# Hybrid encoder trunk, two layers: weight tiles split once per layer, kept in DRAM and reloaded as two parts

## The chip, the core and the metric

The kernel runs on one core of one Trainium2 chip. The metric is device time in microseconds (us) from the first to the last instruction; the kernel before takes 4894.8 us (median of three runs).

## What is computed

An encoder trunk of two layers runs over two sequences of 1024 tokens and 1024 channels. For each layer and each sequence:

```
h     = rms_norm(x, g_pre) * (1 + scale) + shift
proj  = h @ w_in
o_a   = mla_mixer(...) * silu(z_a)        # attention
o_b   = rwkv7_mixer(...)                  # a scan per direction
o_c   = mamba2_mixer(...)                 # chunked scan per direction
o_d   = gated_deltanet_mixer(...)         # chunked delta rule per direction
mixed = concat(o_a, o_b, o_c, o_d)
x     = x + gate * rms_norm(mixed @ w_out, g_post)
```

`shift`, `scale` and `gate` come from a conditioning vector through `w_ada`. `w_in` is repacked on the host to 32 tiles of 128 columns (1024 x 128 numbers each), `w_out` is 1024 x 1024. All inputs and outputs are float32.

## The kernel before, in words

**Units.** A unit is one sequence in one layer; there are four, in the order (sequence 0, layer 0), (1, 0), (0, 1), (1, 1). Each unit has an input projection (`stage_in`), the four mixers, and an output projection (`stage_out`; `stage_out_last` in the last unit). The projections work on halves of 512 tokens. The input projection of the next unit and the output projection of the one before are laid beside the mixers of a unit, so the projections fill TensorE while the mixers' chains run on all engines. Projections of P go through DRAM: `in_tile` stores each 128 x 512 result to the tensor P, from which the mixers load.

**Products of two halves.** Both projections multiply float32 numbers as sums of two parts. The activations are kept as `hh` (a rounded part, type float32r) and `hl` (the rest), made once for a token half. The weights are made into `wh` and `wl` in the same way by `split_w` (lines 324 to 330): a cast on ScalarE (line 327, `wh`) and a subtraction on VectorE (line 329, `wl`). Three products are summed: wh x hh, wh x hl and wl x hh.

**Weight tiles.** One load brings 128 partitions x 512 numbers (256 KB) into a buffer `w`, of which there are two. For `w_in` (`in_tile`, lines 301 to 322) this is half a tile of 128 columns, so two loads, two splits and 24 products of 512 columns for each result; for `w_out` (`out_tiles`, lines 332 to 349) it is a quarter of the rows for 256 columns, with 24 products of 256 columns. `wh` and `wl` have three buffers each. A load has to wait until the split two before it has read its buffer; a split has to wait until TensorE has used the split three before it.

**How often.** Every unit and both token halves load and split all weights of the layer again: 4 units x 2 halves x 64 parts of `w_in` = 512 and 4 x 2 x 16 of `w_out` = 128, so 640 splits for 160 different parts.

**Order of the work.** The instructions are emitted in program order with priorities, and a planner of the framework orders each engine's queue by a simulated timeline. `urgent()` gives the split instructions and the eviction of a result a priority ahead of everything else; `spread`, `behind` and `ahead` spread the priorities of projection steps over those of the mixers. Each engine then runs its queue strictly in that order, and all loads and stores are issued by SyncE (line 144), which waits for a buffer or for data before it issues and holds all that follows it. `paced` (line 458) lets TensorE begin a group of 5 or 8 projection products only after the group before has begun, by way of a tiny write of GpSimd (line 462).

The mixers' lines that are named later: 522 to 537 invert triangular blocks on VectorE (transposes at 522 and 537, the update steps `iT` at 529 and `SC` or `iR` at 530), 551 and 558 merge them on TensorE, and 629 to 640 are a short convolution.

Of the kernel before, what the change touches and what calls it, by code (L numbers as in the profile page):

```python
# [10 lines left out]
F32 = mybir.dt.float32  # L11
F32R = mybir.dt.float32r
# [9 lines left out]
D = 1024  # L22
MIX = 1800
EA = 60
GK = 4
GB = 3
# [4 lines left out]
GL = 3  # L31
# [77 lines left out]
class Body:  # L109
    def __init__(self, ctx, tc, A, outs, sl=None):  # L110
        self.tc, self.nc, self.A, self.outs = tc, tc.nc, A, outs
        self.n = 0
        self.side = "left"
        self.span = None
        nc = tc.nc
        self.cp = ctx.enter_context(tc.tile_pool(name="cp", bufs=1))
        self.dr = ctx.enter_context(tc.tile_pool(name="dr", bufs=1, space=DRAM))
        self.banks = 3
        self.held = None
        self.token = self.t(self.cp, [1, 1], tag="token")  # L120
        self.gate, self.run = None, 0
        self.ident = self.const(self.cp, "ident")
        self.blk = self.const(self.cp, "blk")
        self.bsel = self.const(self.cp, "bsel")
        self.cc = self.t(self.cp, [128, 4], tag="cc")
        nc.vector.memset(self.cc[:, 0:1], -0.5)
        nc.vector.memset(self.cc[:, 1:2], EPS)
        nc.vector.memset(self.cc[:, 2:3], 0.5)
        nc.vector.memset(self.cc[:, 3:4], 1.0)
        self.mhalf, self.eps, self.phalf, self.one1 = (self.cc[:, i:i + 1] for i in range(4))  # L130

    def open_io(self, ctx):
        """the pools of the projections"""
        self.pj = self.pool(ctx, "pj")
        self.sp = self.pool(ctx, "sp", 2)
        self.pps = self.pool(ctx, "pps", 2, PSUM)
# [20 lines left out]
    def sumsq(self, ps, col, sq, n, rhs, w, start=True, stop=True):  # L157
        """ps[:, col:col+w] = per-token sums over the channels of sq[:, 128 n : 128 n + 128]"""
        for x in range(2):
            self.nc.tensor.matmul(ps[64 * x:64 * x + 64, col:col + w], sq[:, n * 128 + 64 * x:n * 128 + 64 * x + 64], rhs,  # L160
                                  start=start, stop=stop)
# [99 lines left out]
    def stage_in(self, s, L, l, xsrc, Pd, parts=((0, W_ORDER), (1, W_ORDER))):  # L261
        """parts: (token half, tiles); the half of the part before is still there"""
        for hf, names in parts:
            if self.held is None or self.held[0] != (Pd, hf):
                self.spread()
                hh = self.t(self.pj, [128, 8, 512], F32R, tag="hh")
                hl = self.t(self.pj, [128, 8, 512], F32R, tag="hl")
                self.norm_in(s, L, xsrc, hf, hh, hl)
                self.held = (Pd, hf), hh, hl
            for name in names:  # L270
                self.spread()
                self.in_tile(l, name, hf, *self.held[1:], Pd)
# [28 lines left out]
    def in_tile(self, l, name, hf, hh, hl, Pd):  # L301
# [4 lines left out]
        for k in range(8):  # L306
            if k % 4 == 0:
                w = self.t(pj, [128, 4, 128], tag="w", bufs=2)
                self.dma(w, self.A["w_in"][l, ci][:, k * 128:k * 128 + 512].rearrange("p (k c) -> p k c", k=4))
            if k % GK == 0:  # L310
                with self.urgent():
                    wh, wl = self.split_w(w[:, k % 4:k % 4 + GK], [128, GK, 128])
            for i, (a, b) in enumerate(((wh, hh), (wh, hl), (wl, hh))):
                self.paced(TK, ps[0:M], a[:, k % GK, 0:M], b[:, k, :], dict(start=(k == 0 and i == 0), stop=(k == 7 and i == 2)))
# [9 lines left out]
    def split_w(self, w, shape):  # L324
        nc, pj = self.nc, self.pj
        wh = self.t(pj, shape, F32R, tag="wh", bufs=GB)
        nc.scalar.copy(wh, w)  # L327
        wl = self.t(pj, shape, F32R, tag="wl", bufs=GL)
        nc.vector.tensor_tensor(wl, w, wh.bitcast(F32), SUB)  # L329
        return wh, wl  # L330

    def out_tiles(self, l, ch, hh, hl, kqs, at=lambda kq: kq):
        """products of 4 token tiles with a quarter of the columns of w_out, over the quarters kqs of its rows"""
        nc, pj = self.nc, self.pj
        pss = [self.t(self.pps, [128, 2, 256], tag="pj") for _ in range(2)]
        for n, kq in enumerate(kqs):
            w = self.t(pj, [128, 2, 256], tag="w", bufs=2)
            self.dma(w, self.A["w_out"][l, ch, kq // 2][:, (kq % 2) * 512:(kq % 2) * 512 + 512].rearrange("p (k c) -> p k c", k=2))
            with self.urgent():
                wh, wl = self.split_w(w, [128, 2, 256])  # L340
            for i in range(4):
                ps = pss[i // 2][:, i % 2]
                c = slice(i * 128, (i + 1) * 128)
                for k in range(2):
                    a, b = hh[:, at(kq) * 2 + k, c], hl[:, at(kq) * 2 + k, c]
                    first, last = n == 0 and k == 0 and i % 2 == 0, n == len(kqs) - 1 and k == 1
                    for m, (u, w2) in enumerate(((a, wh), (a, wl), (b, wh))):
                        self.paced(TO, ps, u, w2[:, k], dict(start=first and m == 0, stop=last and m == 2, skip_group_check=True))
# [51 lines left out]
    def stage_out_last(self, s, L, l, xsrc, od, dst, parts, ctx=None):  # L400
        """the last output in parts (token half, quarters of the rows of w_out, whether the sums begin or end),
        while the mixers of the later quarters still run"""
# [53 lines left out]
    def paced(self, n, *mm):  # L456
        """a matmul of a bulk stream: groups of n, each issued after the group before has begun"""
# [21 lines left out]
    def behind(self, p0, p1, n, fs):  # L479
        """emit fs with priorities spread over those from p0 to p1"""  # L480
# [34 lines left out]
    def invert(self, pool, r, d, src):  # L515
        """r = inverses of the unit triangular 32 x 32 diagonal blocks of src, transposed"""
# [15 lines left out]
    def merge(self, pool, psp, r, d, src, dst):  # L532
        """dst = inverse of the unit triangular 64 x 64 blocks of src from the inverses r of their diagonal blocks"""
# [33 lines left out]
    def pair_t(self, psp, dst, src, scale=None):  # L567
        """dst[(c parity, t), (c // 2, x, e)] = transposes of 8 chunks of both heads of src, times scale[(c parity, t), c // 2, x]"""
# [9 lines left out]
    def dma_pair(self, dst, src, swap):  # L578
        """dst[(x or 1 - x, t), c, e] (DRAM) = src[(c parity, t), (c // 2, x, e)]"""
# [6 lines left out]
    def head_sum(self, ps, sq, n):  # L586
        """ps[half, i] = sums over the channels of the head of the other half"""
# [4 lines left out]
    def heads_back(self, psp, y):  # L592
        """transposes back to channels: y[(1 - x, t), c, pr, e] -> [(pr, e), x, c, t]"""
# [5 lines left out]
    def rows2(self, t, r0, q):  # L599
        """rows r0 to r0 + 256 and quarter q of the tokens"""  # L600
        return t[r0:r0 + 256, q * 256:q * 256 + 256].rearrange("(r p) t -> p r t", r=2)
# [54 lines left out]
    def rwkv_norm(self, p, psp, L, Pd, q, y, yd, bon, od, free):  # L656
        """normalisation, bonus and gate of a quarter of the tokens"""
# [416 lines left out]
    def gdn_norm(self, p, psp, L, Pd, q, y, yd, fq, od, free):  # L1074
        """normalisation and gate of a quarter of the tokens"""
# [422 lines left out]
    def attend(self, p, psp, qd, kd, krd, VO, ot):  # L1498
        """softmax of every head; the maxima of a head are found during the head before"""
# [74 lines left out]
    def mixers(self, L, Pd, l, od, which="dcab"):  # L1574
        """the streams right (d, a) and left (b, c)"""
# [9 lines left out]
    def last_mixers(self, L, Pd, l, od, io):  # L1585
        """three streams: d, c on the right; b; a in the place of the projections"""
# [16 lines left out]
    def full(self):  # L1603
# [32 lines left out]
        def ahead(w, n, f):  # L1636
            """emit f with priorities spread over the next w, n steps"""
# [87 lines left out]
```

## Time and profile before

| | |
|---|---|
| Runs | 4888.07, 4894.8, 4915.18 us |
| Span of the profiled execution (first to last instruction) | 4894.9 us |
| Instructions | 100724 |
| TensorE products / weight loads | 38644 each |
| Mean granted TensorE clock | 0.878 of full speed |
| DMA traffic | 671.79 MB, mean 137 GB/s |
| HBM read / written | 486.53 / 178.57 MB |

The profile's page comes from one execution, whose own time is its span, 4894.9 us; nothing else around it is shown. PE is TensorE, PEld its weight loads (they overlap the products), DVE VectorE, ACT ScalarE, POOL GpSimd, SP SyncE, and a q behind a name is the engine's sequencer, which waits and issues. In a group of instructions "out<-in" are the program's tile names, and behind the bar stand the busy time in us, the mean of one in ns, and the idle time of the engine just before these instructions with what ended it. The chain that ended last is followed back from the last instruction: at each step to what released it, or to the instruction before it on its engine. A wait "A <- B" means that A stood until B was done. Products are pipelined: two that follow each other start 0.23 us apart though each is shown for 0.39 us.

### The profile page before, as it was taken

How to read it: one execution, taken by the hardware profiler on the slowest of the kernel's cores; microseconds unless marked ns; L12 is line 12 of the kernel's file. 1: busy time of each engine (PE TensorE's matmuls, PEld its weight loads, DVE VectorE, ACT ScalarE, POOL GpSimd, SP SyncE). 2: the span in 40 equal slices, each digit the busy share in tenths (PEclk: the TensorE clock that was granted, in tenths of full speed). 3: DMA queues.
4: the chain of work that ended last, by engine and by line, in shares of the span. 5: the costliest groups of instructions: out<-in, count | busy, mean ns of one | idle time of the engine just before them, and what ended most of it. 6: DMA issues, size and time to landing. Idle time of an engine off the chain costs nothing.

```text
span 4894.9 us, 100724 instructions
## 1 busy us (share of the span) xinstructions
PE 4389.3 (90%) x38644; PEld 3358.2 (69%) x38644; DVE 3343.1 (68%) x6837; ACT 2178.9 (45%) x4734; POOL 397.6 (8%) x2093
## 2 busy tenths in 40 slices
PE   6879798999997988999989898899989989898997
PEld 3667576766776776756767667776767766776686
DVE  2488877566578787566459778657546968856666
ACT  2444363563434534443454453455344354344333
POOL 0101010000101000000011100000011100000001
PEclk8889898998997987989989798798889979878788
DMA  4444264242453546363345353545145535455224
GB/s 144 136 148 138 99 192 132 87 131 99 135 171 126 160 127 192 109 197 110 112 154 162 109 174 117 174 139 147 63 133 165 163 111 158 130 181 156 85 86 137
DMA packets 495063, 671.79 MB, mean 137 GB/s; under 512 B 149752, under 2 KB 265976, under 8 KB 493560
## 3 DMA queue, kind: packets, MB, share of 16 engines
q1 hardware_dynamic: 494584, 665.36, 43.6%
q8 instruction: 306, 5.01, 0.4%
q14 instruction: 173, 1.42, 0.1%
HBM read 486.53 MB, written 178.57 MB: 136 GB/s over the span
## 4 chain that ended last, share of the span: by engine, by line
PE 49%; DVE 13%; DMA 10%; issue 3%; ACT 3%; SPq 1%; POOL 0%; DVEq 0%; POOLq 0%; ACTq 0%
PE pj L458 21%; PE b L824 3%; PE b L1568 2%; PE b L551 2%; DVE iA L522 1%; PE b L558 1%; SPq L144 1%; PE b L1456 1%; PE b L1555 1%; PE pj L243 1%; PE w L863 1%; DVE wl L329 1%; DVE GT L537 1%; PE b L1524 1%; PE y L1220 1%
## 5 line engine op out<-in xcount | busy, mean ns | idle before, releaser
L458 PE MATMUL pj<-hh,wl 128*128 128x512 f32 (+1 forms) x2048 | 848.2, 415 | 32.0 <-DVE wl L329 18.4
L458 PE MATMUL pj<-hh,wh 128*128 128x512 f32 (+1 forms) x2048 | 854.6, 418 | 11.9 <-DVE iT L529 3.2
L458 PE MATMUL pj<-hl,wh 128*128 128x512 f32 (+1 forms) x2048 | 849.7, 415 | 16.9 <-POOL token L462 16.6
L327 ACT CAST wh<-w 128x512 fp32r<-128x512 f32 x640 | 395.1, 618 | 775.4 <-PE pj L458 495.1
L329 DVE TENSOR_TENSOR wl<-w,wh 128x512 fp32r<-128x512 f32 x640 | 446.6, 699 | 245.3 <-ACT wh L327 211.8
L458 PEld LDWEIGHTS pj<-hh,wl 128*128 128x128 f32 (+1 forms) x2048 | 397.5, 194 | 137.5 <-issue 20.7
L458 PEld LDWEIGHTS pj<-hh,wh 128*128 128x128 f32 (+1 forms) x2048 | 397.6, 194 | 115.3 <-issue 19.9
L458 PEld LDWEIGHTS pj<-hl,wh 128*128 128x128 f32 (+1 forms) x2048 | 396.9, 194 | 113.0 <-POOL token L462 22.9
L462 POOL MEMSET token<- 1x1 f32 x1613 | 143.7, 89 | 3317.1 <-PE pj L458 3307.1
L458 PE MATMUL pj<-wh,hl 128*128 128x256 f32 x896 | 266.6, 310 | 0.7 <-DVE hl L363 0.5
L458 PE MATMUL pj<-wh,hh 128*128 128x256 f32 x768 | 238.7, 311 | 6.3 <-ACT hh L362 4.1
L1559 ACT ACTIVATE pT<-b 128x512 f32<-128x512 f32 x256 | 149.8, 596 | 210.6 <-PE b L1557 207.4
L458 PE MATMUL pj<-wl,hh 128*128 128x256 f32 x768 | 234.0, 305 | 0.0
L294 PE MATMUL pj<-c_ident,x 128*128 128x128 f32 x416 | 118.8, 388 | 109.9 <-ACT hh L298 41.0
L1525 DVE TENSOR_REDUCE mx<-b 128x1 f32<-128x512 f32 x256 | 169.7, 686 | 68.5 <-PE b L1524 66.8
L638 DVE SCALAR_TENSOR_TENSOR cva<-cvi,cw,cva 128x1024 f32<-128x1024 f32 x144 | 183.9, 1279 | 47.4 <-ACT cva L634 29.3
L458 PEld LDWEIGHTS pj<-wh,hl 128*128 128x128 f32 x896 | 181.3, 207 | 14.2 <-issue 6.2
L296 ACT ACTIVATE ht<-pj,shc,gsc 128x256 f32<-128x256 f32 x208 | 118.4, 569 | 156.6 <-PE pj L294 84.0
L828 DVE SCALAR_TENSOR_TENSOR G<-b,Dk,mk 128x128 f32<-128x128 f32 x512 | 143.8, 344 | 61.9 <-PE b L824 61.1
L1568 PEld LDWEIGHTS b<-VO,pT 128*64 128x64 f32 x4096 | 150.2, 151 | 42.6 <-issue 29.4
L824 PE MATMUL b<-AR,BK 64*64 64x128 f32 x2048 | 176.7, 299 | 0.0
L1568 PE MATMUL b<-VO,pT 128*64 128x65 f32 x4096 | 168.4, 238 | 4.7 <-ACT pT L1559 4.3
(403 smaller groups left out, 9407.1 us busy)
## 6 DMA issues: line engine op xcount, KB each, us to landing
w<-w_in SPq DMA_DIRECT2D x512, 256.0 KB
P<-st SPq DMA_DIRECT2D x248, 256.0 KB
x<-x SPq DMA_DIRECT2D x76, 512.0 KB
w<-w_out SPq DMA_DIRECT2D x128, 256.0 KB
G<-P SPq DMA_DIRECT2D x112, 256.5 KB
cvi<-P SPq DMA_DIRECT2D x48, 512.0 KB
f<-acr SPq DMA_DIRECT2D x32, 512.0 KB
bkc<-bkd SPq DMA_DIRECT2D x64, 256.0 KB
```

The costliest lines, as they stand in the source:

```text
L294: nc.tensor.transpose(ps[:, i * 128:(i + 1) * 128], xs[i][:, k * 128:(k + 1) * 128], self.ident)
L296: nc.scalar.activation(ht, ps[:, 0:256], AF.Identity, scale=L.gsc[:, k, s:s + 1], bias=L.shc[:, k, s:s + 1])
L327: nc.scalar.copy(wh, w)
L329: nc.vector.tensor_tensor(wl, w, wh.bitcast(F32), SUB)
L458: m = self.nc.tensor.matmul(*mm[:3], **mm[3]).ins
L462: t = self.nc.gpsimd.memset(self.token, 0.0).ins
L638: nc.vector.scalar_tensor_tensor(a, c[:, j:j + 1024], wt(j, i), a, MUL, ADD)
L824: nc.tensor.matmul(ps[self.half(x ^ a), i * 128:i * 128 + 128], BK[self.half(x), pr, c, a], AR[self.half(x), pr, c].rearrange("p a t -> p ...
L828: v.scalar_tensor_tensor(G[:, x, pr, c, :], ps[:, i * 128:i * 128 + 128], Dk[:, c, 2 * x + pr:2 * x + pr + 1], mk, MUL, MUL)
L1525: v.tensor_reduce(mx[:, n, qt:qt + 1], ps, AX.X, ALU.max, negate=True)
L1559: nc.scalar.activation(pT[kt], ps, AF.Exp)
L1568: nc.tensor.matmul(po[64 * x:64 * x + 64, i, :], pT[kt][:, o:o + 64], VO[:, kt, h, :], start=(kt == 0 and i == 0), stop=(kt == 7), skip_gr ...
```

## The change

`split_w` goes. A new function `halves` gives both parts of a weight part in one tile `w2` (128 partitions x 2 x 512, 512 KB; three buffers, the same room as `wh` and `wl` had). The first user in a layer loads `w`, splits it into `w2` as before, and stores `w2` to DRAM. Every other user (the other token half, the other sequence) loads `w2` from there. The products, their order and `paced` stay as they are. Which use is the first follows the order of emission: the units 0 and 2 hold all 160 first uses, spread over both of their token halves, and the units 1 and 3 have none. Other lines of the diff only take out comments.

```diff
-GK = 4
-GB = 3
-GL = 3
...
         self.held = None
+        self.kept = {}
+        self.wd = {(n, l): self.t(self.dr, [m, 128, 2, 512], tag=f"w{n}{l}") for l in range(DEPTH) for n, m in (("in", 2 * NWT), ("out", 16))}
...
         for k in range(8):
             if k % 4 == 0:
-                w = self.t(pj, [128, 4, 128], tag="w", bufs=2)
-                self.dma(w, self.A["w_in"][l, ci][:, k * 128:k * 128 + 512].rearrange("p (k c) -> p k c", k=4))
-            if k % GK == 0:
-                with self.urgent():
-                    wh, wl = self.split_w(w[:, k % 4:k % 4 + GK], [128, GK, 128])
-            for i, (a, b) in enumerate(((wh, hh), (wh, hl), (wl, hh))):
-                self.paced(TK, ps[0:M], a[:, k % GK, 0:M], b[:, k, :], dict(start=(k == 0 and i == 0), stop=(k == 7 and i == 2)))
+                w2 = self.halves(("in", l, ci, k // 4), lambda: self.A["w_in"][l, ci][:, k * 128:k * 128 + 512]).rearrange("p u (k c) -> p u k c", k=4)
+            for i, (a, b) in enumerate(((0, hh), (0, hl), (1, hh))):
+                self.paced(TK, ps[0:M], w2[:, a, k % 4, 0:M], b[:, k, :], dict(start=(k == 0 and i == 0), stop=(k == 7 and i == 2)))
...
-    def split_w(self, w, shape):
+    def halves(self, key, src):
         nc, pj = self.nc, self.pj
-        wh = self.t(pj, shape, F32R, tag="wh", bufs=GB)
-        nc.scalar.copy(wh, w)
-        wl = self.t(pj, shape, F32R, tag="wl", bufs=GL)
-        nc.vector.tensor_tensor(wl, w, wh.bitcast(F32), SUB)
-        return wh, wl
+        w2 = self.t(pj, [128, 2, 512], F32R, tag="w2", bufs=3)
+        wf = w2.bitcast(F32)
+        if key in self.kept:
+            self.dma(wf, self.kept[key])
+            return w2
+        w = self.t(pj, [128, 512], tag="w", bufs=2)
+        self.dma(w, src())
+        with self.urgent():
+            nc.scalar.copy(w2[:, 0], w)
+            nc.vector.tensor_tensor(w2[:, 1], w, wf[:, 0], SUB)
+        kept = self.wd[key[:2]]
+        self.kept[key] = kept[key[2] * 2 + key[3]] if key[0] == "in" else kept[key[2] * 4 + key[3]]
+        self.dma(self.kept[key], wf)
+        return w2
...
         for n, kq in enumerate(kqs):
-            w = self.t(pj, [128, 2, 256], tag="w", bufs=2)
-            self.dma(w, self.A["w_out"][l, ch, kq // 2][:, (kq % 2) * 512:(kq % 2) * 512 + 512].rearrange("p (k c) -> p k c", k=2))
-            with self.urgent():
-                wh, wl = self.split_w(w, [128, 2, 256])
+            w2 = self.halves(("out", l, ch, kq), lambda: self.A["w_out"][l, ch, kq // 2][:, (kq % 2) * 512:(kq % 2) * 512 + 512]).rearrange("p u (k c) -> p u k c", k=2)
...
-                    for m, (u, w2) in enumerate(((a, wh), (a, wl), (b, wh))):
-                        self.paced(TO, ps, u, w2[:, k], dict(start=first and m == 0, stop=last and m == 2, skip_group_check=True))
+                    for m, (u, x) in enumerate(((a, 0), (a, 1), (b, 0))):
+                        self.paced(TO, ps, u, w2[:, x, k], dict(start=first and m == 0, stop=last and m == 2, skip_group_check=True))
```

## Rows read from the trace of the kernel before

**Rows 1.** The page: span; busy time of each engine, share of the span, instructions.
```profile
span 4894.9 us, 100724 instructions
...
PE 4389.3 (90%) x38644; PEld 3358.2 (69%) x38644; DVE 3343.1 (68%) x6837; ACT 2178.9 (45%) x4734; POOL 397.6 (8%) x2093
```

**Rows 2.** The page, the chain that ended last, by engine, then by line.
```profile
...
PE 49%; DVE 13%; DMA 10%; issue 3%; ACT 3%; SPq 1%; POOL 0%; DVEq 0%; POOLq 0%; ACTq 0%
PE pj L458 21%; PE b L824 3%; PE b L1568 2%; PE b L551 2%; DVE iA L522 1%; PE b L558 1%; SPq L144 1%; PE b L1456 1%; PE b L1555 1%; PE pj L243 1%; PE w L863 1%; DVE wl L329 1%; DVE GT L537 1%; PE b L1524 1%; PE y L1220 1%
```

**Rows 3.** Groups by line: shapes and count, busy us and mean ns, idle before.
```profile
...
L329 DVE TENSOR_TENSOR wl<-w,wh 128x512 fp32r<-128x512 f32 x640 | 446.6, 699 | 245.3 <-ACT wh L327 211.8 <-PE pj L458 23.7 <-PE b L571 2.5
...
L327 ACT CAST wh<-w 128x512 fp32r<-128x512 f32 x640 | 395.1, 618 | 775.4 <-PE pj L458 495.1 <-DMA w<-w_in 189.0 <-issue 32.9
```

**Rows 4.** Waits, whole span: engine, line, waited for, us in total, times, longest.
```profile
...
ACT wh L327 <- PE pj L458: 495.1, 273, 9.4
...
DVE wl L329 <- ACT wh L327: 211.8, 151, 7.5
...
ACT wh L327 <- DMA w<-w_in: 189.0, 94, 8.7
```

**Rows 5.** Stretches from 360, 1440, 1680, 2640, 2880, 3840, 4080: all engines; L329 alone.
```profile
...
sum 840.00, PE 740.32 PEld 596.53 DVE 768.81 ACT 330.87 POOL 90.76; mean PE 105.76 PEld 85.22 DVE 109.83 ACT 47.27 POOL 12.97
...
sum 840.00, DVE 111.24; mean DVE 15.89
```

**Rows 6.** The chain from 3850 to 3920: shares by line; pieces (start, us, what).
```profile
...
by line: PE pj L458 35.3%; DVE wl L329 9.9%; DVE iT L529 9.8%; issue 9.3%; DVE SC L530 8.9%; PE yd L1347 5.8%; DMA w<-w_in 4.1%; DVE f L1328 3.6%; DVE st L319 2.7%; PE cb L1321 2.6%; DVE f L1330 1.9%; DVE xd L1340 1.7%; DVE t L1359 1.4%; DV
...
3886.45 0.41 DVE iT L529
3886.86 0.60 DVE wl L329
3887.46 0.33 DVE SC L530
...
3908.10 0.63 ACT wh L327
```

**Rows 7.** The page, DMA queue: packets, MB, share of 16 engines.
```profile
...
q1 hardware_dynamic: 494584, 665.36, 43.6%
```

**Rows 8.** A dense stretch: all engines, granted clock, DMA share, GB/s; L329 alone.
```profile
...
2520.00:2640.00 120.00, 110.96 (x685) 89.17 (x684) 93.57 (x143) 62.52 (x90) 17.74 (x86) 0.96 0.57 174
...
2520.00:2640.00 120.00, 19.22 (x28) 0.96 0.57 174
```

**Rows 9.** The chain's longest pieces: DMAs, start, us, what.
```profile
...
3167.59 5.90 DMA x<-o
...
3780.69 5.42 DMA w<-w_in
...
3905.11 2.88 DMA w<-w_in
...
4326.42 3.44 DMA x<-o
```

**Rows 10.** Timeline of TensorE: the same product of two tiles, start, us.
```profile
...
2584.61 0.40 PE L458 MATMUL pj<-hl,wh 128*128 128x512 f32 x1
...
2587.34 0.39 PE L458 MATMUL pj<-hl,wh 128*128 128x512 f32 x1
```

**Rows 11.** SyncE's waits, whole span: us in total, times, longest.
```profile
...
SPq L144 <- DVE wl L329: 527.3, 217, 21.4
```

**Rows 12.** The chain's longest pieces: products in a row, first and last of eight.
```profile
...
1420.36 12.78 PE pj L458 x55
...
3843.29 11.59 PE pj L458 x50
```

**Rows 13.** Tile w: issue of its DMA, ns min/median/max, first and last start.
```profile
...
L144 SPq DMA_DIRECT2D w<-w_in x512: 327/333/1487, 8.5 to 4132.8; - x171
```

## Prediction

> **What bounds the kernel now.** I read the page's busy times first. TensorE is busy for 90% of the span, VectorE for 68%, ScalarE for 45% [rows 1]. VectorE is no bound over the whole span, but the chain that ended last says that it matters: TensorE 49% of the span, VectorE 13%, DMAs 10%, ScalarE 3% [rows 2]. The shares of that row add up to 79%, because the chain can't be followed back over the first part of the span; a share of the chain is therefore divided by 0.79 here where the whole span is meant. Then the groups by line: splitting a weight tile costs a cast on ScalarE of 618 ns and a subtraction on VectorE of 699 ns, 640 times each, 395 and 447 us in all [rows 3]. Then the waits: the cast and the subtraction also hold their queues. ScalarE stood 495 us at a cast for TensorE to give back a buffer, and 189 us for the weights' DMA; VectorE stood 212 us at a subtraction for the cast [rows 4]. Last the stretches. In seven of 120 us each VectorE is busy for 769 of 840 us (92%), more than TensorE's 740, and 111 us of it are splits [rows 5]. There VectorE is the bound, and the chain shows how: in one of them it runs from a triangular inverse's step to a split to the next step, and the splits are 9.9% of it [rows 6].
>
> **What goes.** The keys are layer, tile and part, so of 640 splits 160 stay: w_in has 2 layers x 32 tiles x 2 parts = 128 keys, w_out 2 x 4 x 4 = 32. 480 casts (297 us of ScalarE) and 480 subtractions (336 us of VectorE) go, three quarters of each. What that is worth:
> - The subtraction is 1% of the span on the chain (49 us), 62 us after division by 0.79; three quarters are **-46 us**. The bounds: 0, if everything beside it ends as late, and -336, all of it.
> - The cast is not among the chain's named lines. Where the chain is spelled out it has one piece of 0.63 us while the splits' share of that 70 us is 9.9% (6.9 us) [rows 6], so some 9% of the 62 us: 5.6, of which three quarters go, **-4 us** (0 to -46, as if it were the subtraction).
> - The held queues: three quarters of VectorE's 212 us are 159. On the chain VectorE has 13%/0.79 = 16% of the span while it is busy for 68%, so about 24% of its time is on the path: **-38 us** (0 to -159). ScalarE's larger holds I count at nothing more: it is 45% busy and has 3% of the chain, so what is late next behind it is TensorE itself.
>
> Together -88 us.
>
> **What comes.** A later user now loads both halves, 512 KB for 256. 480 x 0.262 MB are 126 MB more read; 160 stores of 0.524 MB are 84 MB written; 210 MB in all. The queue moved 665 MB in 43.6% of its 16 engines' span [rows 7], which is 3.2 us of all engines for a MB, so the share becomes 57%, and 3.2 x 0.262 = 0.84 us is what the extra 256 KB takes.
> - *Other transfers behind the weights.* In the densest stretch 28 tiles pass in 120 us [rows 8]: at 0.84 us a load they fill 24 us of it now (20%), at 1.68 us they fill 47 later (39%). A transfer that comes at random meets a load with that chance and waits half of it out: 0.20 x 0.42 = 0.08 us now, 0.39 x 0.84 = 0.33 us later, so 0.25 us more; at the mean of 16 tiles in 120 us (640 over the span) it is 0.14. DMAs have 10% of the chain, 490 us, in pieces of some 4 us [rows 9], so 120 pieces, 150 after division by 0.79: 21 to 38 us. I take **+25** (0 to 126: each of the 150 behind a whole further 256 KB).
> - *Weights that come late.* So far five buffers stand between DMA and TensorE, two raw and three split. A kept load goes straight into one of three, so it can be issued when the tile three back has been used. Where TensorE runs projections alone, the same point of the next tile comes 2.73 us later [rows 10]; two tiles are 5.5 us of cover. Loads of 512 KB (x from the mixers' output) have pieces of 3.4 to 5.9 us on the chain, weight loads of 256 KB 2.9 to 5.4 [rows 9], the issue on SyncE within them. That is just covered, and no longer where SyncE holds the load for a microsecond: its queue is in order, and it already stands 527 us in 217 waits for the subtraction to free a raw buffer [rows 11], which becomes a wait for TensorE's last product with a tile. Queued behind are stores of P, and the mixers' loads and stores. Bursts without cover are few: eight pieces of the chain have 40 to 55 such products of 512 columns, from the first to the last shown [rows 12]; at 12 to a tile that is some ten tiles beyond the third, 12 over the span. At 1 us each that is 12; I take **+20**, since some bursts follow each other closely. The far end is the row nearest to a late load, 189 us at the cast [rows 4], until now hidden by the split buffers: three quarters, +142. The lower end is 0.
> - *The stores.* 160 issues on SyncE of 0.33 us, as a weight load's [rows 13], are 53 us in a queue that mostly waits: nothing, for 1% of the chain is SyncE's. A store keeps its buffer until it has landed, about 5 us against 2.7 us of products; the two other buffers cover this, and if they don't, the ten or so dense tiles pay 2.3 us each, +23.
> - *Order.* The planner orders every queue anew once instructions go. No row of one program prices that; I count it at nothing, and it is one more reason for a range with ends on both sides.
>
> **The sum.** -88 + 25 + 20 = -43 from the profiled span of 4894.9 us, which stands within 0.1 us of the median of the three runs, 4894.8; nothing measurable lies around it. Forecast **4852 us**, by itself 4810 to 4885: both costs at 0 give 4807, the traffic's high end of 38 with twice the late weights 4885. A change under 0.5% (24 us) can't be told from none here.
>
> **Rivals.**
> 1. *Slower: weights late at TensorE.* TensorE takes its products in order, so a late tile stops the mixers' products behind it as well; this decides once a load, SyncE's hold included, needs over 6.5 us, one above the cover. For it: the densest stretches already run the DMA engines at 57% [rows 8], loads of 256 KB already took up to 5.4 us, and the load's place in SyncE's queue is behind waits of 2.4 us (527/217). Against: on average a tile there comes every 4.3 us (120/28), which gives 8.6 us of cover. Price: +142 late, +38 traffic, -88: **4987**.
> 2. *No change: TensorE is the bound.* The engine is busy for 90%, and what VectorE gives back would only become slack. The Trainium skill (Perfetto Trace Analysis, Identifying Performance Opportunities) says that improving a kernel generally means improving its most-contended engine; by that VectorE's relief is worth nothing. The trace agrees over the whole span and disagrees in the seven stretches, where VectorE is the busier. Half of the -88 would be left, against +45: **4896**.
> 3. *More: the seven stretches shrink by all that leaves them.* Three quarters of 111 us is 83, beside the 38 of held queues, and with +25 of traffic: -96, **4799**. For it VectorE's 92%; against it TensorE's 740 of 840 us in the same stretches.
>
> That tiles would be split again after all is excluded by the keys. That a load waits for other tiles' stores is part of rival 1; loads of P run today while other rows of it are stored, which speaks against it.
>
> **Chances.** Forecast 0.36, rival 1 0.30, rival 2 0.18, rival 3 0.16. Faster by over 0.5% are rival 3 and most of the forecast (0.28): 0.44. Within 0.5%: the rest of the forecast and most of rival 2: 0.21. Slower: rival 1 and the remainder of rival 2: 0.35. Since cases of both signs hold most of it, the range takes in all of them: 4770 (rival 3 with the traffic at 0, 4774, rounded down) to 4990 (rival 1).
>
> **What the changed profile would show.** The cast and the subtraction x160 each; VectorE near 3007 us busy and ScalarE near 1882; 210 MB more and a DMA share near 57%. Right: TensorE's idle time behind VectorE falls, the seven stretches' kin get shorter, VectorE's share of the chain drops by 2 to 3 points, and TensorE's products wait for kept loads for under 30 us in all. Wrong: TensorE or its weight loads wait for the new tile's DMA for 100 us or more, or the DMAs' share of the chain rises by over 3 points.

## The result, and the profile after

The kernel after took 5102.2 us (median of four runs, 5083.3 to 5119.8) beside 4891.4 for the kernel before (4876.0 to 4915.2): a ratio of **1.0418**, 95% interval 1.038 to 1.0457, some 205 us slower. Here and below a ratio leaves out executions in a slower state of the chip (one each in e7, e16 and e17, whose medians still include it). The profiled execution has a span 186.6 us longer than the one before. In the kernel after, the tiles `w` and `w2` and the constants that feed products all appear as "w", and the kept tensors as "win" and "wout". Product line 458 is now 460, the DMA line 144 is 143.

The page after: span, busy times, DMA queue, and the groups of the split (beside [rows 1], [rows 7] and [rows 3]).

```profile
span 5081.5 us, 99496 instructions
...
PE 4523.7 (89%) x38644; PEld 3397.1 (67%) x38644; DVE 3071.8 (60%) x6357; ACT 1915.9 (38%) x4254; POOL 396.1 (8%) x2093
...
q1 hardware_dynamic: 517624, 875.08, 53.9%
...
L330 ACT CAST w<-w 128x512 fp32r<-128x512 f32 x160 | 98.9, 619 | 229.0 <-DMA w<-w_in 105.1
L331 DVE TENSOR_TENSOR w<-w,w 128x512 fp32r<-128x512 f32 x160 | 113.3, 710 | 114.3 <-ACT w L330 103.8
```

The change did what it says: 160 casts and subtractions are left, VectorE is busy for 271 us less, ScalarE for 263 us less, and 210 MB more pass through the queue. TensorE is busy for 134 us *more* with the same 38644 products. A product is shown for 0.39 us where the next can start after 0.23 us, so a short gap between two products counts as busy, and most of the loss (134 of 187 us) has no wait of its own. Where it lies is seen when the span is cut at the projections. These are the stretches of the kernel before from the first to the last of the 1536 products of 512 columns of each unit, those products alone (columns: start and end, length, busy products and weight loads, granted clock, DMA share, GB/s):

```profile
88.00:792.00 704.00, 415.18 (x1536) 292.68 (x1536) 0.88 0.46 144
850.00:1738.00 888.00, 417.27 (x1536) 283.69 (x1536) 0.93 0.43 132
2299.00:3014.00 715.00, 408.37 (x1536) 284.24 (x1536) 0.89 0.44 139
3446.00:4172.00 726.00, 418.41 (x1536) 285.12 (x1534) 0.90 0.43 134
```

The same stretches of the kernel after:

```profile
91.00:865.00 774.00, 420.85 (x1536) 290.85 (x1536) 0.88 0.62 201
908.00:1870.00 962.00, 446.18 (x1536) 292.79 (x1535) 0.91 0.52 163
2456.00:3169.00 713.00, 425.91 (x1536) 291.14 (x1536) 0.89 0.63 206
3628.00:4377.00 749.00, 427.84 (x1536) 289.50 (x1536) 0.89 0.56 179
```

The last product of a unit's input projection comes at 865, 1870, 3169 and 4377 us in place of 792, 1738, 3014 and 4172: later by 73, 132, 155 and 205. The span is 187 longer at its end. So the loss is gathered up to the last input projection, the larger part of it in the first two units, and the last unit's mixers give a little back. The mean granted clock of a stretch differs by at most 0.02.

Not all of this comes from wider loads, as the first two units of two runs of the next section show. First e3, the kernel before with loads of 512 KB, then e9, the kernel after with loads of 256 KB and five buffers:

```profile
92.00:803.00 711.00, 410.57 (x1536) 288.40 (x1534) 0.89 0.60 188
872.00:1895.00 1023.00, 442.57 (x1536) 297.30 (x1536) 0.89 0.50 154
...
92.00:824.00 732.00, 418.78 (x1536) 290.69 (x1536) 0.89 0.52 164
894.00:1864.00 970.00, 439.95 (x1536) 292.46 (x1536) 0.90 0.42 125
```

Unit 0's projection ends at 864 to 866 us in three orders of the kernel after (e8 and e12 beside it), at 787 to 792 in the kernel before (with e5 to e7), at 800 and 803 in the kernel before with wide loads (e14, e3), and at 824 and 826 in e9 and e13. So wide loads alone explain little of unit 0; its stores and its three buffers come into question, and no run parts them. Unit 1's stretch is 970 us long in e9 and 961 in e13, nearly as in the kernel after, though their loads are as small as before: it gets that long without wider loads.

Now the waits. SyncE, whole span, after (beside [rows 11]; in us, times, longest):

```profile
SPq L143 <- PE pj L460: 1076.6, 401, 25.7
...
SPq L143 <- DVE w L331: 140.6, 59, 14.7
```

and all that TensorE's products waited for a kept load, with the first two of its other waits:

```profile
PE b L553 <- DVE mT L544: 66.1, 17, 9.0
PE pj L293 <- DVE x L288: 42.5, 20, 6.7
PE pj L460 <- DMA w<-win: 39.9, 25, 5.1
```

Of the 401 waits 350 (1031 us) stand before one of the 480 kept loads: TensorE was still using the buffer that the load was to fill. The rest stand before other transfers. That SyncE waits so often doesn't by itself mean that three buffers are too few: with five buffers (e9) it waits 991 us in 399 times. TensorE itself shows only 40 us behind the kept loads, its weight loads 24 us, in part in the same standstills. The longest of the 25 looks like this. SyncE from 1402 us on, in order of time:

```profile
1405.59 2.41 SPq L143 DMA_DIRECT2D f<-gcr  x4
1408.58 0.33 SPq L143 DMA_DIRECT2D w<-win  x1
...
1413.96 0.32 SPq L143 DMA_DIRECT2D w<-win  x1
1416.89 0.32 SPq L143 DMA_DIRECT2D P<-st  x1
1419.23 0.32 SPq L143 DMA_DIRECT2D w<-win  x1
```

and TensorE's products beside it, with the DMA queue from 1402 to 1422 us as the third line:

```profile
1414.82 0.39 PE L460 MATMUL pj<-hh,w 128*128 128x512 f32 x1
1420.30 0.79 PE L460 MATMUL pj<-hh,w 128*128 128x512 f32 x1 [5.09 <-DMA w<-win]
...
q1 hardware_dynamic: 2424, 4.86, 93.2%
```

Four loads of 512 KB (`f`) for a mixer had just been issued, and the DMA engines were 93.2% busy for 20 us. The kept load that TensorE waited for is the one issued at 1408.58: the last update of the semaphore that the product waited for comes at 1420.26, 11.7 us later. The cover of two tiles was 5.5 us. This load is the slowest of all. From the issue to the last such update the 480 kept loads take 4.0 us in the median, four fifths of them 3.2 to 6.3 us, and 86 of them more than 5.5; the 640 weight loads of the kernel before take 2.9 us in the median, 2.5 to 4.5 us, and 25 more than 5.5. The stop has a second cost: the granted clock is 1.00 from 1402 to 1415 us and 0.51, the lower of the two levels (1.2 GHz), from 1420 to 1426 us, after the stop, and the products there start 0.43 us apart instead of 0.23.

### The profile page after: what moved, and what is told of

It reads as the page before. It is cut to its first block, busy times and chain, and to the rows that moved or that the text cites. A ratio compares the mean times of both kernels' runs of the same rounds, so it can differ in the third digit from the quotient of the medians.

```text
span 5081.5 us, 99496 instructions
## 1 busy us (share of the span) xinstructions
PE 4523.7 (89%) x38644; PEld 3397.1 (67%) x38644; DVE 3071.8 (60%) x6357; ACT 1915.9 (38%) x4254; POOL 396.1 (8%) x2093
## 3 DMA queue, kind: packets, MB, share of 16 engines
q1 hardware_dynamic: 517624, 875.08, 53.9%
## 5 line engine op out<-in xcount | busy, mean ns | idle before, releaser
L460 PE MATMUL pj<-hh,w 128*128 128x512 f32 (+1 forms) x4096 | 1457.1, 426 | 77.5 <-DMA w<-win 39.9
L460 PEld LDWEIGHTS pj<-hh,w 128*128 128x128 f32 (+1 forms) x4096 | 794.5, 198 | 302.3 <-issue 51.2
L460 PE MATMUL pj<-hl,w 128*128 128x512 f32 (+1 forms) x2048 | 865.0, 423 | 17.0 <-POOL cvi L631 7.9
L460 PEld LDWEIGHTS pj<-hl,w 128*128 128x128 f32 (+1 forms) x2048 | 406.8, 199 | 112.3 <-POOL token L464 11.7
L460 PE MATMUL pj<-w,hh 128*128 128x256 f32 x1536 | 354.8, 316 | 13.5 <-ACT st L374 6.7
L460 PEld LDWEIGHTS pj<-w,hh 128*128 128x128 f32 x1536 | 270.2, 207 | 41.7 <-issue 17.3
L460 PE MATMUL pj<-w,hl 128*128 128x256 f32 x960 | 266.9, 310 | 9.7 <-ACT hl L426 3.9
L460 PEld LDWEIGHTS pj<-w,hl 128*128 128x128 f32 x960 | 184.0, 206 | 24.4 <-issue 4.5
L331 DVE TENSOR_TENSOR w<-w,w 128x512 fp32r<-128x512 f32 x160 | 113.3, 710 | 114.3 <-ACT w L330 103.8
L826 PEld LDWEIGHTS b<-AR,BK 64*64 64x64 f32 x2048 | 134.6, 142 | 65.3 <-issue 48.2
```

The source lines that it names most:

```text
L331: nc.vector.tensor_tensor(w2[:, 1], w, wf[:, 0], SUB)
L460: m = self.nc.tensor.matmul(*mm[:3], **mm[3]).ins
L826: nc.tensor.matmul(ps[self.half(x ^ a), i * 128:i * 128 + 128], BK[self.half(x), pr, c, a], AR[self.half(x), pr, c].rearrange("p a t -> p ...
```

## The experiments

All ratios are to the kernel before, measured beside each run. The kernels are the one before or the one after with one edit.

| | from | edit | us | ratio, 95% interval |
|---|---|---|---|---|
| e5 | before | `MIX` 1800 to 1782 | 4940.6 | 1.0095 [1.0070, 1.0119] |
| e6 | before | `ED` 90 to 89 | 4940.0 | 1.0096 [1.0064, 1.0127] |
| e7 | before | 4 KB of room unused | 4928.9 | 1.0048 [1.0017, 1.0080] |
| e18 | before | 8 KB of room unused | 5619.7 | 1.1467 [1.1415, 1.1519] |
| e8 | after | `MIX` 1782 | 5037.9 | 1.0295 [1.0272, 1.0318] |
| e12 | after | `ED` 89 | 5072.0 | 1.0335 [1.0264, 1.0406] |
| e3 | before | 512 KB a load | 5101.3 | 1.0380 [1.0341, 1.0418] |
| e14 | before | e3 with `MIX` 1782 | 5103.2 | 1.0420 [1.0366, 1.0475] |
| e17 | before | 480 splits more | 5070.5 | 1.0339 [1.0284, 1.0394] |
| e10 | before | three tiles deep | 5581.2 | 1.1391 [1.1323, 1.1459] |
| e2 | after | 256 KB a load, 3 buffers | 5074.4 | 1.0342 [1.0300, 1.0385] |
| e9 | after | 256 KB a load, 5 buffers | 4977.4 | 1.0146 [1.0107, 1.0184] |
| e13 | after | e9 with `MIX` 1782 | 4995.0 | 1.0188 [1.0145, 1.0231] |
| e4 | after | kept loads on ScalarE | 5038.6 | 1.0276 [1.0236, 1.0316] |
| e11 | after | 4 buffers | 5107.1 | 1.0416 [1.0372, 1.0461] |
| e1 | after | 5 buffers | 5551.0 | 1.1314 [1.1287, 1.1341] |
| e15 | after | 5 buffers until unit 3 | 5348.3 | 1.0921 [1.0877, 1.0964] |
| e16 | after | parts of half the size, 6 buffers | 5338.5 | 1.0873 [1.0814, 1.0932] |

**First look: buffers, bytes, whole loads (e1 to e4).** e1 gives the kept tiles five buffers.

```diff
-        w2 = self.t(pj, [128, 2, 512], F32R, tag="w2", bufs=3)
+        w2 = self.t(pj, [128, 2, 512], F32R, tag="w2", bufs=5)
```

> The changed kernel with five buffers for the two parts instead of three (8 KB more of each partition), nothing else. Depth (a kept load can be issued only when the tile three back has been used, so it comes late at TensorE and holds SyncE's queue meanwhile): back to 4850 to 4930, SyncE's waits for TensorE's projection products from 1077 us to under 500, TensorE's waits for kept loads from 64 us (weight loads included) to under 20. Traffic (210 MB more slow every other transfer): stays at 5050 to 5120. Order (the planner's new order of every queue is the worse one, by itself): anything, most likely 5000 to 5100, with SyncE's waits down.

It took 5551 us, far slower than the kernel after and outside every range given. Two more buffers are also 8 KB more of room in each partition; e18 below shows that the room is the reason.

e2 stores and reloads the rounded part alone, 256 KB, and uses it in the third product too; it leaves out the second part of the weights in the products. The subtraction is still made, into a scratch tile.

```diff
-        w2 = self.t(pj, [128, 2, 512], F32R, tag="w2", bufs=3)
+        w2 = self.t(pj, [128, 512], F32R, tag="w2", bufs=3)
...
-            nc.scalar.copy(w2[:, 0], w)
-            nc.vector.tensor_tensor(w2[:, 1], w, wf[:, 0], SUB)
+            nc.scalar.copy(w2, w)
+            nc.vector.tensor_tensor(self.t(pj, [128, 512], F32R, tag="wl", bufs=2), w, wf, SUB)
```

> The changed kernel, but only the rounded part is stored and reloaded (256 KB a load as before the change), and stands in for the rest in the third product; casts, subtractions, products, number of loads and three buffers stay. It leaves out the second part of the weights. Depth: the load is shorter by 0.84 us only, so 5000 to 5080. Traffic: 126 MB of the loads and half of the stores go, so 4880 to 4950. Order: 5000 to 5100.

5074 us: with three buffers, half the bytes win little or nothing over the kernel after's three orders (5038 to 5102).

e3 leaves the kernel before as it is, with all its 640 splits and its five buffers, but each weight load brings 512 KB, of which half is used.

```diff
-                w = self.t(pj, [128, 4, 128], tag="w", bufs=2)
-                self.dma(w, self.A["w_in"][l, ci][:, k * 128:k * 128 + 512].rearrange("p (k c) -> p k c", k=4))
+                w = self.t(pj, [128, 8, 128], tag="w", bufs=2)
+                self.dma(w, self.A["w_in"][l, ci].rearrange("p (k c) -> p k c", k=8))
```

> The kernel before, each of its 640 weight loads bringing 512 KB of which half is used; buffers, splits and queues as before, 168 MB more read. Depth: five buffers still stand before TensorE, so 4890 to 4930. Traffic: 640 loads of 512 KB against the change's 480 and 160 stores, so nearly the whole loss, 5030 to 5100. Order: the planner sees longer loads, 4850 to 4950.

5101 us, as much as the kernel after. The waits of ScalarE and VectorE at the split in e3 (beside [rows 4]), and its DMA queue:

```profile
ACT wh L327 <- DMA w<-w_in: 304.1, 143, 15.0
DVE wl L329 <- ACT wh L327: 301.1, 197, 7.0
...
q1 hardware_dynamic: 494584, 833.13, 52.5%
```

The cast's wait for its load rose from 189 to 304 us and its longest from 8.7 to 15 us. 168 MB more in the weights' loads, with nothing else changed but 4 KB of room, cost 3.8%; the room alone is 0.5% (e7). The total is that of the kernel after, but not the make-up. The mean granted clock of the profiled execution is 0.856 in e3 (0.865 in e14), beside 0.878 in the kernel before and 0.875 in the kernel after: part of what wide loads cost in the old kernel is a slower TensorE, which the kernel after hardly has.

e4 issues the kept loads from ScalarE's queue, so that they no longer stand in SyncE's.

```diff
-            self.dma(wf, self.kept[key])
+            nc.scalar.dma_start(out=wf, in_=self.kept[key])
```

> The changed kernel with the kept loads issued by ScalarE's queue instead of SyncE's, three buffers. If it is the holding of SyncE's queue alone (all other loads and stores behind a wait for a buffer): 4880 to 4980, since ScalarE is 38% busy, though its evictions and mixers' steps now stand behind those waits. Depth: the load still comes late at TensorE and holds a queue, 5050 to 5200. Traffic: 5080 to 5150.

SyncE's longest waits in e4:

```profile
SPq L143 <- ACT st L316: 454.1, 119, 18.5
SPq L143 <- PE pj L293: 239.5, 31, 49.5
```

The 1077 us of waiting for TensorE are gone from SyncE's queue, and the time is 5039 us, within the spread that other orders of the kernel after have (e8, 5038). The hold is moved and not removed: the kept loads now wait in ScalarE's queue, and SyncE waits 454 us for ScalarE's evictions. That the holding of SyncE's own queue is the main cause is not borne out.

**The planner's order (e5 to e8, e12).** Small edits that change no work, but move priorities or room:

```diff
-MIX = 1800
+MIX = 1782
...
-ED = 90
+ED = 89
```

> The kernel before with the width MIX over which the projections' priorities are spread at 1782 instead of 1800 (1% less): no work, byte or buffer changes, only the order that the planner finds. Order (the kernel before sits in an order that happens to be a good one, and any change of the program loses it): 4960 to 5100. Depth or traffic or held queues (the loss is the change's own): within 0.7% of before, 4860 to 4930.

> The kernel before with ED (where the laid-in projections of a unit end, in per cent of its mixers) at 89 instead of 90, nothing else. Order: 4960 to 5100, and another value than the run with MIX at 1782. The change's own loss: 4860 to 4930.

> The kernel before with 4 KB of each partition taken by an unused tile in the projections' pool (and one one-element write on GpSimd), nothing else: the room that the wide loads before took more, without their bytes. Room (less SBUF keeps the next mixer's buffers from opening early): 5030 to 5110, as the wide loads, and the five buffers' 5551 for 8 KB is the same cause. Traffic: 4880 to 4930, and the wide loads' loss was their bytes. Order: 4960 to 5100, not to be told from room by this run alone.

> The changed kernel with MIX at 1782 instead of 1800, nothing else. Order: 4880 to 5120, off from the changed kernel's 5102 by more than 25 us, to either side. The change's own loss: 5070 to 5130.

> The changed kernel with ED at 89 instead of 90, nothing else: a third draw of the planner's order, beside 5102 and 5038. Loss of the change's own of some 135 us beside a spread of order of some 50: 5030 to 5110. Loss of order alone: a value under 5000 becomes likely.

The kernel before lost 0.5 to 1.0% each time; its own order is the best of the four seen. The kernel after won 0.8 to 1.2% each time; its own order is the worst of three. 4940 us lies between the two ranges that were given for e5 and e6. With the same edit in both, the change costs 2.0% with `MIX` at 1782 (e8 against e5) and 2.4% with `ED` at 89 (e12 against e6), beside 4.2% without one. So some 2 to 3% (100 to 145 us) belong to the change itself, as far as three orders tell, and the rest of the 4.2% to the two orders that happened to be compared.

**Bytes again, and the number of buffers (e14, e9, e13, e10).** e14 is e3 in another order; e9 is e2 with five buffers and one scratch tile, in the room of the kernel before; e13 is e9 in another order; e10 is the kernel before with one raw buffer and two of each part.

```diff
-GB = 3
+GB = 2
...
-GL = 3
+GL = 2
...
-                w = self.t(pj, [128, 4, 128], tag="w", bufs=2)
+                w = self.t(pj, [128, 4, 128], tag="w", bufs=1)
```

> The kernel before with 512 KB loads of which half is used, and MIX at 1782: a second draw beside its 5101. Bytes cost what the change costs, with all splits and five buffers still there: 5050 to 5150. An unlucky order: 4930 to 5000.

> The half-bytes kernel (only the rounded part kept and reloaded, 256 KB a load, leaving out the second part of the weights) with five buffers instead of three, and one scratch buffer for the subtraction instead of two; 16 KB of a partition in all, as before the change. Depth: the cover is back, the bytes are not there, so the relief of VectorE and ScalarE shows: 4840 to 4930. Relief worth nothing, and depth no cause: 5030 to 5090, as with three.

> The half-bytes kernel with five buffers and MIX at 1782: a second draw of the planner's order beside its 4977, to be set against 4929 to 4941 of the three moved kernels before (it leaves out the second part of the weights). It has the same bytes a load and as many buffers as the kernel before, and three quarters of the splits are gone. Relief worth what the prediction took (88 us): 4830 to 4880. Relief worth nothing: 4920 to 5000.

> The kernel before with one raw buffer and two for each split part instead of two and three (the loads of w_ada keep two of their own): three tiles between DMA and TensorE, as in the change; bytes, splits and loads stay. Depth: 5040 to 5150, against 4936 for the two runs whose priorities alone were moved. Traffic: 4900 to 4960.

e14 repeats e3 (1.042). Against the moved orders of before the wider loads cost 2.8 to 3.7% (1.0380 less 1.0096, 1.0420 less 1.0048), and 3.2% in the same order (e14 against e5). From e2 to e9, two more buffers at 256 KB a load win 2.0%, to e13 1.5%, which is little more than what an order alone can do.

e10 loses 13.9%, far more than was expected, but it changes more than the depth. With one raw buffer only one weight load can be under way at a time, where the kernel after has room for two beside the tile in use. SyncE and TensorE's products in e10:

```profile
SPq L144 <- DMA w<-w_in: 384.7, 196, 6.6
...
PE pj L458 <- ACT wh L327: 168.6, 153, 6.0
```

SyncE stood until a weight load had landed, and TensorE until the cast behind it was done; neither row is among the long ones of the kernel after. So e10 shows that the kernel before needs its loads to overlap, and not what three buffers cost in the kernel after. The bytes of a load have a price in the old kernel; that the number of loads ahead has one in the kernel after is not shown. What e9 and e13 show besides: with the loads' old size, five buffers and 480 splits fewer, the kernel is still no faster than before (1.0146 and 1.0188 beside 1.0080 for the mean of e5 to e7). 4995 us for e13 lies in the range that was given for a relief worth nothing.

**More buffers in the kernel after (e11, e15, e16).** e11 has four buffers; e15 five, in a pool of their own that is closed before unit 3's late projections, three from there on; e16 six of half the size, with loads of 256 KB that hold both parts of 256 numbers a partition.

```diff
+            self.wp.close()
+            self.pw, self.nw = self.pool(io, "pw"), 3
```

> The changed kernel with four buffers for the two parts instead of three: 4 KB more of each partition, which cost the kernel before some 30 us at most (run with the pad). Depth: 4950 to 5030. Traffic: 5040 to 5130. Room: over 5130, on the way to five buffers' 5551.

> The changed kernel with five buffers for the two parts up to the last unit, then three: in the run with five throughout the projections of the first two units ended 74 us earlier than before the change, and the loss lay behind the last unit's projections. Cover (bytes wait for buffers): 4880 to 4980. Room (8 KB keep the mixers' buffers from opening in every unit): over 5100.

> The changed kernel with parts of half the size (256 KB for both halves of 256 columns) in six buffers, the same bytes and the same room for them; a load can be issued when half a tile's products are done, so its cover is five half tiles, 6.8 us, instead of two tiles, 5.5. Cover: 4960 to 5040. Bytes whatever the cover: 5040 to 5110. Issue on SyncE, now twice as many: over 5110.

None helps. Four buffers change nothing that can be measured (5107 us), though they take 4 KB more of room. e16 doubles the number of loads, and SyncE's wait grows with it:

```profile
SPq L143 <- PE pj L461: 1213.8, 705, 14.4
```

It also makes 320 splits of half the size and takes 2 KB more of room; what of its loss each of these is was not parted.

**What splits cost, and what room costs (e17, e18).** e17 does the split of the 480 later uses in the kernel before twice, the second time into tiles that nothing reads.

```diff
+        if key in self.seen:
+            dh = self.t(pj, shape, F32R, tag="dh", bufs=1)
+            nc.scalar.copy(dh, w)
+            nc.vector.tensor_tensor(self.t(pj, shape, F32R, tag="dl", bufs=1), w, dh.bitcast(F32), SUB)
+        self.seen.add(key)
```

> The kernel before, in which each of the 480 later uses of a weight tile casts and subtracts it a second time, into a scratch tile that nothing reads (4 KB of room; 480 casts and 480 subtractions more, no byte of DMA more). What the 480 splits cost is thus measured from the other side. Beside the 4929 to 4941 us that moved priorities or a pad of 4 KB alone give: if the -88 us of relief that I predicted were the price of 480 splits, their doubling costs about as much again, 5000 to 5060. If VectorE's and ScalarE's splits hide beside TensorE's work, the doubling costs under 50 us: 4900 to 4985, and there was no relief to be had.

The page of e17, busy times and the two added groups:

```profile
PE 4435.2 (88%) x38644; PEld 3392.4 (67%) x38644; DVE 3624.4 (72%) x7317; ACT 2435.7 (48%) x5214; POOL 404.1 (8%) x2093
...
L333 ACT CAST dh<-w 128x512 fp32r<-128x512 f32 x480 | 296.4, 618 | 356.4 <-DMA w<-w_in 227.9
L334 DVE TENSOR_TENSOR dl<-w,dh 128x512 fp32r<-128x512 f32 x480 | 332.7, 693 | 170.3 <-ACT dh L333 168.4
```

e17's ratio is 2.9% (142 us) above that of the pad of 4 KB that it includes, and its time (5050 to 5083 us in three executions) is about the upper end of the range given for a price. 480 more splits have a price, although TensorE is busy for 88% and VectorE for 72%. The Trainium skill (Perfetto Trace Analysis, Identifying Performance Opportunities) says that improving a kernel generally means improving its most-contended engine; rival 2 took from it that work on the other engines is worth nothing. e17 doesn't bear that reading out: work added to less busy engines cost 2.9%. The run doesn't say how much of the 142 us is VectorE's time itself: the second split also holds the raw tile longer, and so delays the next load.

e18 takes 8 KB of room in the kernel before and does nothing with it.

```diff
+        self.nc.gpsimd.memset(self.t(self.pj, [128, 2048], tag="pad")[0:1, 0:1], 0.0)
```

> The kernel before with an unused tile of 8 KB a partition in the projections' pool, which is the room that two more buffers of 512 KB took. If the room is what made five buffers lose in the second half (the last unit's streams get fewer buffers or wait for room that is given back), this kernel loses like it: 5300 to 5560, with the loss after 3400 us. If it was the order of loads in five buffers, the room costs little: 4900 to 4960.

5620 us. The kernel loses as e1 does, and with the same waits. SyncE in e18, two of its waits:

```profile
SPq L145 <- DVE mT L543: 274.0, 19, 70.4
...
SPq L145 <- ACT mr L1534: 113.0, 16, 30.1
```

TensorE's products in e18:

```profile
PE pj L459 <- ACT hh L363: 130.3, 8, 45.5
```

The same three of e1 (SyncE, SyncE, TensorE):

```profile
SPq L143 <- DVE mT L544: 248.0, 19, 70.4
...
SPq L143 <- ACT mr L1535: 127.4, 16, 30.4
...
PE pj L460 <- ACT hh L364: 133.9, 7, 45.2
```

Room was what e1 lost. At equal room, e1 (1.1314) stands *below* e18 (1.1467), by about 1.3%. That is the one comparison in which the change wins, in a schedule that is bound elsewhere and with one order of each, so it shows neither a size nor surely the direction. I can't say which tile or pool of the last unit goes without at 8 KB, nor why giving the room back in e15 didn't mend its last part; that wasn't traced.

**Where TensorE's time went.** TensorE's waits, added up over all rows of its list by what ended them, beside its busy time, in the profiled execution of each run (us):

| | busy | waits for DMAs | waits for VectorE | mean clock | span |
|---|---|---|---|---|---|
| before | 4389 | 47 | 278 | 0.878 | 4895 |
| after | 4524 | 90 | 254 | 0.875 | 5082 |
| e5 (before, `MIX`) | 4436 | 36 | 281 | 0.869 | 4957 |
| e8 (after, `MIX`) | 4504 | 81 | 238 | 0.875 | 5021 |
| e6 (before, `ED`) | 4437 | 46 | 278 | 0.870 | 4963 |
| e12 (after, `ED`) | 4478 | 72 | 266 | 0.883 | 5029 |
| e3 (before, 512 KB) | 4547 | 52 | 289 | 0.856 | 5103 |
| e9 (after, 256 KB, 5 buffers) | 4475 | 47 | 255 | 0.867 | 4988 |

From before to after, e5 to e8 and e6 to e12 the waits for DMAs rise by 43, 46 and 26 us and those for VectorE fall by 24, 43 and 12: they nearly cancel. The loss is in the busy time, which rises by 134, 69 and 41. The mean clock doesn't explain that, for it is higher in e8 and e12 than in e5 and e6. A smaller thing can be counted: of the 6144 products of 512 columns, 322, 352 and 365 start at the lower clock in before, e5 and e6, and 504, 512 and 490 in after, e8 and e12. There they start about 0.44 us apart instead of 0.24, so some 150 more of them cost about 30 us (an estimate). What the rest of the busy time is stays open.

No version here beats the kernel before.

## Why the prediction was wrong

The forecast was 4852 us, the range ended at 4990, and the result is 5102, on the other side of the kernel before.

- **Counts and busy times: nearly right.** 160 splits, 210 MB. ScalarE at 1916 us was forecast at 1882, VectorE at 3072 at 3007: the splits went as counted (446.6 to 113.3 us on VectorE, 333 less), but other work of VectorE took 62 us longer. The DMA share is 53.9% for 57%, over a longer span.
- **Relief, -88: not found in the result, and not refuted as a price.** e17 shows that 480 splits more cost 142 us, so 88 was no overestimate of what such work can cost. TensorE's waits for VectorE do get shorter, as was announced, by 12 to 43 us. But e9 and e13, in which as many splits go and the loads keep their size and number of buffers, are not faster than the moved orders of before: e13 is 0.9% slower than e5, which has the same `MIX`. What the change does besides widening the loads can't be read from the difference to the wide loads either: it is +0.4% with `MIX` at 1800 (1.0418 beside 1.0380) and -1.3% at 1782 (1.0295 beside 1.0420), which an order alone can do.
- **What comes, +20 for weights that come late and +25 for other transfers behind them: the step that failed.** The sum priced what a late tile makes the chain wait and put the rest of the supply at nothing. As waits the 45 were about right: TensorE's waits for DMAs rose by 26 to 46 us. But the cost of wider loads is not only such waits. In e3 and e14 the runs measured 139 to 182 us for 512 KB a load with the five buffers of the kernel before (against e5 to e7), while TensorE's waits for DMAs in e3 are 52 us, hardly more than in the kernel before. In the kernel after, TensorE is busy for 41 to 134 us longer with the same products, and the sum has no term for that. The suppositions on the load itself held on the whole: the median of 4.0 us is under the cover of 5.5, and 86 of 480 loads exceed it. How much of the change's own loss is its wider loads, its three buffers or its stores stays open; e3 loses little in unit 0 and runs at a lower clock. e3 holds late weights and other transfers together, so no run parts +20 from +25.
- **Stores, 0.** Not tried alone. Unit 0, in which half of the input projection's parts are split and stored, ends its projection 73 us late in the kernel after, and in all three orders. Wide loads alone make it 8 to 16 us late (e3, e14), the stores with five buffers and small loads 32 to 39 (e9, e13); whether its stores or its three buffers do the rest wasn't parted. So 0 may have been too little here.
- **Order, counted at nothing.** It was 0.5 to 1.0% for the kernel before, 24 to 47 us, and a loss in all three edits, since its own order is the best one seen. The forecast missed by 250 us: 88 of relief not found, 94 to 137 too little for what comes (if e3's price is the change's) and 24 to 47 of order make 206 to 272.
- **The rivals.** Rival 1 had the sign right and came nearest, at 4987, 115 short. That its +142 for late weights lies in the 139 to 182 measured for wide loads is luck: it was taken from ScalarE's wait at the cast, it has another +38 for traffic beside it, and TensorE's wait for the kept loads, which it was to be, is 40 us. Its sign (100 us or more of such waits) did not come, nor did that of the forecast (under 30). Both were tied to waits, and the loss is mostly not in waits. The announced shares of the chain can't be read: in the kernel after it can be followed back over less than a fifth of the span.
- **Rival 2** (4896) and **rival 3** (4799) are out by the number. What rival 2 said of the relief, that it would become slack, is near to what e9 and e13 show; its reason, that TensorE is the bound, doesn't fit e17.

## What to carry to other kernels

Trading compute for traffic in a stream that feeds the busiest engine is not priced by the waits that a profile shows alone: here they nearly cancelled, and the kernel was still 2 to 4% slower. A test that widens the loads of the old kernel gives a first price before the change is written; compare then the stretches and the granted clock too, for an equal total is no equal cause. Where a planner orders the queues, move one priority by a hundredth in both kernels and see what the order alone is worth. An added buffer also takes room, so run the old kernel with that room left unused beside it.

## What the runs showed of the hardware and the program that I had not expected

- A weight load of 256 KB took 2.9 us in the median in the kernel before, a kept load of 512 KB 4.0 us in the kernel after; the slowest took 11.7 us, where the DMA engines were 93.2% busy over 20 us. The mean share in that unit's projection stretch was 52%.
- After TensorE had stood for 5.09 us, the granted clock was 0.51 for the next 6 us, and products of 512 columns started 0.43 us apart instead of 0.23.
- TensorE's busy time rose by 134 us at the same 38644 products, while its waits for the kept loads add up to 40 us: the busy time isn't work alone.
- 8 KB of unused room cost 14.7%, 4 KB 0.5%.
